# Seven quadrant products in both layers' output projections of a two-layer hybrid trunk on one core

## The chip, the core and the metric

The kernel runs on one core of a Trainium2 chip. The metric is the time of one execution in device microseconds (us), the median of several runs. The engines of the core run their own instruction queues side by side: TensorE (PE; PEld is its weight load), VectorE (DVE), ScalarE (ACT), GpSimd (POOL) and SyncE (SP, which here issues most DMA transfers; POOL issues a few).

## The reference

x is 512 tokens x 1024, fp32, and two layers run one after the other. Cut to what matters:

```python
def hybrid_layer(x, ...):
    h = rmsnorm(x, norm_g)
    p = h @ w_in                                  # 1024 x 3488
    (cq, ckv, kr, g_a, c_h, c_b, c_c, g_b, sg_u, sg_v, g_c, mq, mk, mv, g_d) = split(p)
    o_a = latent attention of cq, ckv, kr         # MLA, 4 heads
    o_b = c_b * short_conv(c_c * c_h, conv_w)
    o_c = spatial_gate(sg_u, sg_v, ...)
    o_d = block-sparse attention of mq, mk, mv    # MoBA, 4 heads
    y = concat([o_a * silu(g_a), o_b * silu(g_b), o_c * silu(g_c), o_d * silu(g_d)])
    return y @ w_out                              # 1024 x 1024

for l in range(2):
    x = x + hybrid_layer(x, ...)
```

The change concerns the last product, y @ w_out, and what leads from it into the next layer's h.

## The kernel before, in words

**Products.** An fp32 product is made of three passes in a rounded format (fp32r): each operand is split into a high part and a low rest, and `mm3` (L253) adds hi·hi, hi·lo and lo·hi into one accumulator. ACT makes the high part (a copy), DVE the low one (a subtraction): `split2` (L246). The activations stand transposed, features on the 128 partitions and the 512 tokens along the row: hT (tags hh0, hl0, hh1, hl1: two halves of 1024 features, each high and low) for the input projection, and y in eight tiles of 128 features x 512 tokens (`y_tiles`, L834): tiles 0 and 1 come from MLA, 2 and 3 from the convolution, 4 and 5 from the spatial gate, 6 and 7 from MoBA.

**Weights.** They are cut into units of 512 KB (`add_unit`, L295). `load_units` (L357) loads them on the SP queue into two raw buffers and `split_units` (L372) splits each in two halves of 128x512 into six pairs of split buffers (`whi`, `wlo`), in the order of use and up to four units ahead of it.

**Order of work.** Nothing is scheduled by the compiler. At build time a planner (`Order`, L66) runs coroutines: the main one (`main`, L1306) emits PE's matmuls and advances a modelled time, and chains spawned by it (`Chain`, L150) emit the work of ACT, DVE, POOL and the transfers when the modelled time of their inputs has come. What it emits is a fixed program order for each engine; on the chip each engine then goes through its own queue in order. A buffer is taken from `Slots` (L112) and given back, an `Event` holds a chain until another has passed a point. So an edit in one place shifts the order on all engines.

**One layer.** PE runs first the low-rank columns (tile cq, 4 token tiles), then `SEQ` (L335): sq (spatial gate's v and MoBA's q), ga0, ga1, kv (MoBA's k and v), su0 to gc1 (the features of convolution, gates and spatial gate). Between these matmuls stand the heads of MLA and MoBA (`mla_heads`, L1120; `moba_heads`, L1166), each with its transposes, scores and outputs. Then comes the output projection.

**Output projection, layer 0.** Eight products, tile "o": for each half of the 1024 output columns and each of the four token tiles, eight y tiles of three passes into one accumulator of 128x512: 2 x 4 x 8 x 3 = 192 matmuls of 128x512. After a token tile's second half `out_chain` (L1237) adds the residual, starts the sum of squares for the next norm and spawns `pre_norm` (L589) of the next layer, which scales the row by its norm (DVE, tile h), transposes it on PE (tile hT, 4 transposes per half) and splits it into hTh and hTl.

**Output projection, layer 1.** Seven products (`seven`, L1328), the method of Strassen and Winograd on 2 x 2 quadrants: y's quadrants are token halves (columns 0:256 and 256:512 of a y tile) by feature halves (`K0` = tiles 2, 3, 0, 1 and `K1` = 4, 5, 6, 7), w_out's quadrants b11, b12, b21, b22 are feature halves by halves of the output columns. `ZPROD` gives the order: b11, t3, b21, t4, t2, t1, b22, each named for its weights; t1 to t4 are sums of weight quadrants. Each product has two row blocks of four feature tiles of three passes: 24 matmuls of 128x512, 168 in all, in the tiles oz, ox, oy, and ot for the last row block. What it needs beside:
- weight sums: `t_sums` (L316) copies a quadrant within DRAM (8 copies of 512 KB on SP, L322) and adds another onto it (8 accumulating transfers issued by POOL, L328). It is spawned for layer 1 when layer 0's MLA heads are done (end of `mla_heads`).
- sums of y quadrants: `put_y` (L838) subtracts the two token halves of a K0 tile in place (DVE), so that t3's left operand stands in the tile, and stores every y tile in DRAM (`ysc`). `s_chain` (L855), once for each pair of a K0 and a K1 tile, loads both back, makes three sums of 256 columns on DVE (tiles ys) and splits them into `sums`: S for t2, S4 for b22 (one pair of tiles with 512 columns) and S for t1 (a second pair with 256 columns). These lie in the buffers of hT, which is free by then.
- outputs: `z_out` (L1276) adds or subtracts a product to or from the residual rows (DVE), and `row_done` (L1257) ends a row: in layer 1 the store.

**Parameters.** `load_params` (L522) loads a layer's small vectors (norm gains, convolution weights and so on) in 14 transfers on SP, `load_norm_gain` (L513) the gain of the input norm. Layer 1's are loaded in the middle of layer 0's projection, after the first group of token tiles.

**Waiting between layers.** `pre_norm` of layer 1 writes hT only after `h_done` of layer 0, an event set when layer 0 no longer needs the buffers of hT.

Of the kernel before, what the change touches and what calls it, by code (L numbers as in the profile page):

```python
# [18 lines left out]
P = 128  # L19
# [180 lines left out]
def hybrid_trunk(ctx: ExitStack, tc: tile.TileContext, x, positions, norm_g, w_c, w_f, w_t, w_o, mla_q_norm_g,  # L200
# [115 lines left out]
    def t_sums(l):  # L316

        for steps in ((("t1", "b11", "b12"), ("t3", "b12", "b22")), (("t2", "t1", "b22"),), (("t4", "t2", "b21"),)):
            for n, a, _ in steps:
                for j in range(2):  # L320
                    o.clk["D"] = max(o.clk["D"], o.now) + 1500.0
                    nc.sync.dma_start(z_src(l, n, j), z_src(l, a, j))  # L322
                    yield o.now + 4000.0
            yield o.now + 4000.0
            for n, _, b in steps:
                for j in range(2):
                    o.clk["G"] = max(o.clk["G"], o.now) + 1000.0
                    nc.gpsimd.dma_start(z_src(l, n, j), quad(l, b, j), accum_op=ALU.add, max_dma_last_dim=1024)  # L328
                    yield o.now + 4000.0
            yield o.now + 8000.0  # L330

# [25 lines left out]
    def load_units():  # L357
        for u in order:
            ch = Chain(o)
            u.raw_slots = rawS  # L360
            if u.name in ("c2_0", "c3_0") or u.name[:-3] in ZPROD and u.name[-3] == "1":
                u.raw_slots = tkS
                u.raw = (yield from tkS.get(ch, f"raw_{u.name}", 96)).rearrange("p a b c -> p (a b c)")
            else:
                u.raw = yield from rawS.get(ch, u.name)
            dma(ch, P * u.a * u.b * 4, u.raw[:, :u.a * u.b], u.src)
            o.set(u.loaded, ch.t)
            for e in LOAD_HOOKS.pop(u.name, ()):
                e()
            yield o.now  # L370
# [179 lines left out]
    for l in range(DEPTH):  # L550
        L = Layer()
        L.l = l
        L.ng_ev = Event()
        L.hT = [[Event(), Event()] for _ in range(NT)]
        L.xss = [cst.tile([P, 4], F32, name=f"xss{t}_{l}") for t in range(NT)]
        L.qd = [Event() for _ in range(NT)]
        L.kd = [Event() for _ in range(NT)]
        L.stat = [Event() for _ in range(NT)]
        L.Vt, L.Mt, L.gates, L.gate_ev, L.MD = {}, {}, {}, {}, {}
        L.md_ev = {n: [Event() for _ in range(NT)] for n in ("mq", "mk", "mv")}  # L560
        L.vt_ev = [Event() for _ in range(NT)]
# [6 lines left out]
        L.hT_free, L.h_done, L.h = Event(), Event(), {}  # L568
# [20 lines left out]
    def pre_norm(L, t, xx, t0, release):  # L589
# [18 lines left out]
        def half(c):  # L608
            c2 = Chain(o, tps[c])
            tp = yield from trS.get(c2, f"hT{t}_{c}_{L.l}")  # L610
            for k in range(4):
                kt = c * 4 + k
                yield from c2.pe(109.0, PE.transpose, tp[:, k * P:(k + 1) * P], h[:, kt * P:(kt + 1) * P], ident)
            hput(c2)
            if L.l:
                yield from c2.wait(layers[L.l - 1].h_done)
            if c not in L.h:
                L.h[c] = [big.tile([P, 4, S], F32R, tag=f"h{x}{c}", name=f"hT{x}{c}_{L.l}") for x in "hl"]
            yield from split2(c2, *(z[:, :, t * P:(t + 1) * P] for z in L.h[c]), tp.rearrange("p (k n) -> p k n", k=4))
            trS.put(c2)  # L620
            o.set(L.hT[t][c], c2.t)
# [216 lines left out]
    def put_y(ch, L, kt, yv):  # L838
# [16 lines left out]
    def s_chain(L, kk):  # L855

        ch = Chain(o)
        for kt in (K0[kk], K1[kk]):
            yield from ch.wait(L.y[kt])
            ch.t = max(ch.t, L.left["y", kt])  # L860
        yield from ch.wait(L.hT_free)
        w = []
        for kt in (K0[kk], K1[kk]):
# [3 lines left out]
        a, b = w  # L867
        ch.t = max(ch.t, c2.t)
        yield from ch.dve(V.tensor_tensor, b[:, 256:512], b[:, 256:512], a[:, 256:512], op=ALU.add)
        yield from ch.dve(V.tensor_tensor, b[:, 0:256], b[:, 0:256], b[:, 256:512], op=ALU.subtract)  # L870
        c2 = Chain(o, ch.t)
        yield from ch.dve(V.tensor_tensor, a[:, 0:256], a[:, 0:256], b[:, 256:512], op=ALU.subtract)
# [32 lines left out]
    def gc_chain(j):  # L905
        def f(L, a, t0):
# [4 lines left out]
            t2S.put(ch)  # L911
        return f


# [205 lines left out]
    def mla_heads(L):  # L1120
# [116 lines left out]
    def out_chain(L, half, t, a, t0, c0=0, c1=512):  # L1237
# [10 lines left out]
        elif half == 1:  # L1248
# [57 lines left out]
    def main():  # L1306
# [20 lines left out]

        def seven(L):  # L1328
            l = L.l
            L.sums = [[big.tile([P, 4, n], F32R, tag=f"h{x}{i}", name=f"sum{x}{i}_{l}") for x in "hl"]  # L1330
                      for i, n in enumerate((512, 256))]
            o.set(L.hT_free, o.now + PELAT)
            us = {}

            def left(n, kk, i):
                c = i * P
                if n in ("t2", "b22"):
                    z, ev = [y[:, kk, (256 if n == "t2" else 0):] for y in L.sums[0]], L.s[n][kk]
                elif n == "t1":
                    z, ev = [y[:, kk, :] for y in L.sums[1]], L.s[n][kk]  # L1340
                else:
                    kt = (K0 if n in ("b11", "t3") else K1)[kk]
                    z, ev = [y[:, (256 if n in ("t3", "t4") else 0):] for y in y_tiles(L, kt)], L.y[kt]
                return z[0][:, c:c + P], z[1][:, c:c + P], ev

            def prod(n, i, a, first, c0=0, c1=512):
# [20 lines left out]
            for n in ZPROD:  # L1367
                for i in range(2):
# [25 lines left out]
            o.set(L.h_done, o.now)  # L1394

        early_put(m)
        for L in layers:
# [19 lines left out]
            for n in SEQ:  # L1417
                if n in TOKS:
                    us = []
                    for t in range(NT):  # L1420
# [17 lines left out]
            if L.seven:  # L1438
                yield from seven(L)
            else:  # L1440
                o.set(L.h_done, o.now)
            for half in range(0 if L.seven else 2):
                us = {}

# [43 lines left out]
    def start():  # L1488
# [52 lines left out]
        hS.put(ch)  # L1541
        o.set(L0.ng_ev, ch.t)

    o.spawn(start())
    o.run()

# [49 lines left out]
```

## Time and profile before

| what | value |
|---|---|
| median of 3 runs | 502.64 us (502.39 to 503.83) |
| the profiled execution's own time | 504.06 us |
| its span in the trace | 502.4 us, so 1.66 us lie outside the span |
| mean granted TensorE clock | 0.999 |
| DMA | 67.30 MB in 28267 packets, mean 134 GB/s |
| transfers on the hardware queue | 37.1% of 16 engines' span |
| transfers issued by POOL | 5.8% of 16 engines' span |

How to read the profile. The page gives each engine's busy time and its share of the span, then the span in 40 slices of 12.56 us, one digit for the busy tenths of each. The chain that ended last is followed back from the last instruction to whatever released it; its shares by engine say which engine set the time. The waits list an engine's idle time by what ended it. Groups of instructions are given by line, engine, operation and tile (out<-in), with the number of instructions, the busy time, the mean ns of one, and the idle time ahead of them. Since the helpers issue nearly everything, the line is mostly that of a helper (L161 for ACT, DVE and POOL, L187 for PE, L264 for loads), and the tile's name tells the work apart. The windows give each engine's busy time between two moments.

### The profile page before, as it was taken

To read this page: it belongs to the slowest core of one execution; us is meant where nothing else is said; L and a number is where in the kernel's file an instruction comes from. 1 tells how busy PE (TensorE), PEld (TensorE's weight loads), DVE (VectorE), ACT (ScalarE), POOL (GpSimd) and SP (SyncE) were. 2 spreads that over 40 slices of the span, in tenths; PEclk is the share of its full clock that TensorE was granted. 3 is DMA by queue.
4 is the path that set the end of the run, shared out by engine and by line. 5 is a ranking of instruction groups with operands and counts; after the bars stand their busy time and mean duration, and the time that the engine had idled before them with its cause. 6 is when DMAs were issued, how large, how long until landed. Compare 5 with 4: busy or idle time off the path is not lost.

```text
span 502.4 us, 7746 instructions
## 1 busy us (share of the span) xinstructions
PE 492.6 (98%) x2472; PEld 417.1 (83%) x2472; DVE 368.7 (73%) x958; ACT 307.2 (61%) x913; POOL 145.8 (29%) x329
## 2 busy tenths in 40 slices
PE   6899999999999999999999999999999999999997
PEld 3798888888888888888889988888888888888886
DVE  4877985458888888544466889777878888765982
ACT  4788755556687766433346896566767587524640
POOL 5867884454011100100311458532240000000000
PEclk9999999999999999999999999999999999999999
DMA  7543414111277722965854422230115312465752
GB/s 266 151 138 99 134 63 142 46 65 43 61 233 207 172 84 88 289 214 165 202 179 130 127 85 84 85 127 1 64 56 180 102 43 105 173 246 185 267 171 89
DMA packets 28267, 67.30 MB, mean 134 GB/s; under 512 B 6593, under 2 KB 11969, under 8 KB 28098
## 3 DMA queue, kind: packets, MB, share of 16 engines
q1 hardware_dynamic: 23970, 62.61, 37.1%
q0 software_dynamic: 4256, 4.20, 5.8%
q8 instruction: 19, 0.31, 0.2%
q14 instruction: 22, 0.18, 0.1%
HBM read 60.51 MB, written 14.68 MB: 150 GB/s over the span
## 4 chain that ended last, share of the span: by engine, by line
PE 91%; POOL 3%; DVE 2%; DMA 2%; ACT 1%; issue 1%; POOLq 0%; DVEq 0%
PE kv L187 10%; PE o L187 9%; PE cq L187 6%; PE sq L187 5%; PE cc L187 4%; PE gb L187 4%; PE cb L187 4%; PE gd L187 4%; PE ch L187 4%; PE su L187 4%; PE gc L187 4%; PE sa L187 3%; PE ga L187 3%; PE oy L187 3%; PE ox L187 2%; PE oz L187 2%
## 5 line engine op out<-in xcount | busy, mean ns | idle before, releaser
L161 ACT ACTIVATE pha<-pTa 128x512 fp32r<-128x512 f32 (+3 forms) x32 | 13.9, 434 | 21.0 <-PE pTa L187 20.8
L161 ACT ACTIVATE pa<-pa,mna 128x256 f32<-128x256 f32 (+3 forms) x45 | 23.9, 539 | 4.1 <-DVE mna L161 4.0
L187 PE MATMUL kv<-whi_kv,hTh 128*128 128x512 f32 x64 | 26.0, 406 | 0.0
L161 ACT ACTIVATE pd<-pd,mnd 128x256 f32<-128x256 f32 (+3 forms) x46 | 24.5, 546 | 1.2 <-DVE mnd L161 0.8
L187 PE MATMUL kv<-whi_kv,hTl 128*128 128x512 f32 x64 | 25.1, 392 | 0.0
L161 ACT ACTIVATE phd<-pTd 128x512 fp32r<-128x512 f32 (+3 forms) x32 | 13.9, 436 | 18.2 <-PE pTd L187 18.0
L187 PE MATMUL kv<-wlo_kv,hTh 128*128 128x512 f32 x64 | 24.9, 390 | 0.0
L187 PE MATMUL cq<-whi_c,hTh 128*128 128x416 f32 x64 | 23.8, 372 | 0.9 <-ACT hTh L161 0.9
L187 PE MATMUL cq<-whi_c,hTl 128*128 128x416 f32 x64 | 22.6, 353 | 0.1
L187 PE MATMUL cq<-wlo_c,hTh 128*128 128x416 f32 x64 | 22.4, 351 | 0.0
L161 DVE CUSTOM_DVE_ANT_0 pa<-sa,maskb 128x512 f32<-128x512 f32 (+3 forms) x32 | 15.0, 484 | 8.2 <-PE pTa L187 5.1
L328 POOL DMA_DIRECT2D t<-in_w_o_dram x8 | 8.8, 1153 | 37.3 <-DMA t<-t 37.2
L161 ACT ACTIVATE hTh<-hT 128x512 fp32r<-128x512 f32 x16 | 9.3, 597 | 16.7 <-PE hT L187 16.6
L187 PE MATMUL sq<-yTh,hTh 128*128 128x512 f32 x48 | 18.9, 393 | 0.0
L187 PE MATMUL o<-whi_wo,yTh 128*128 128x512 f32 x48 | 18.8, 391 | 0.0
L187 PE MATMUL sq<-yTh,hTl 128*128 128x512 f32 x48 | 18.7, 390 | 0.0
L187 PE MATMUL sq<-yTl,hTh 128*128 128x512 f32 x48 | 18.7, 390 | 0.0
L187 PE MATMUL o<-whi_wo,yTl 128*128 128x512 f32 x48 | 18.7, 389 | 0.0
L187 PE MATMUL o<-wlo_wo,yTh 128*128 128x512 f32 x48 | 18.7, 389 | 0.0
L161 DVE TENSOR_TENSOR pld<-pTd,phd 128x512 fp32r<-128x512 f32 (+3 forms) x32 | 15.4, 486 | 4.3 <-ACT phd L161 4.0
L161 DVE TENSOR_TENSOR pla<-pTa,pha 128x512 fp32r<-128x512 f32 (+3 forms) x32 | 15.4, 484 | 4.1 <-ACT pha L161 3.9
L161 DVE CUSTOM_DVE_ANT_0 pd<-sd,maskb 128x256 f32<-128x256 f32 (+3 forms) x32 | 15.1, 484 | 1.0 <-PE pTd L187 0.8
(385 smaller groups left out, 1823.2 us busy)
## 6 DMA issues: line engine op xcount, KB each, us to landing
raw_sq<-in_w_t_dram SPq DMA_DIRECT2D x8, 512.0 KB, 3.5
raw_kv<-in_w_t_dram SPq DMA_DIRECT2D x8, 512.0 KB, 3.5
t<-in_w_o_dram POOLq DMA_DIRECT2D x8, 512.0 KB, 8.1
raw_wo<-in_w_o_dram SPq DMA_DIRECT2D x8, 512.0 KB, 3.6
raw_t<-t SPq DMA_DIRECT2D x8, 512.0 KB, 3.6
raw_c<-in_w_c_dram SPq DMA_DIRECT2D x8, 416.0 KB, 4.1
raw_b<-in_w_o_dram SPq DMA_DIRECT2D x6, 512.0 KB, 4.1
raw_ga<-in_w_f_dram SPq DMA_DIRECT2D x4, 512.0 KB, 3.6
```

Of the source, the lines that this page charges most:

```text
L161: f(*a, **k)
L187: f(*a, **k)
L328: nc.gpsimd.dma_start(z_src(l, n, j), quad(l, b, j), accum_op=ALU.add, max_dma_last_dim=1024)
```

## The change

- `SEVEN` becomes (0, 1): layer 0's output projection runs as seven products too. With it layer 0 gets 14 weight units for its projection (8 before), its weight sums, its y-tile stores and sums, and its output rows end in the order of `z_out`; layer 1's first tiles (`torder`) go in the order 2, 3, 0, 1.
- Layer 0's weight sums are spawned at 36 us of the planner's time (`TS0`), layer 1's after layer 1's sq, no longer at the end of layer 0's MLA heads. A weight unit that reads a sum waits in the planner for that sum (`tsum_ev`).
- y tile 5, the last to be made, is used in place: it is not stored in DRAM and loaded back, its own tile goes to `s_chain` (`own`).
- The sums of `s_chain` lie in one pair of tiles (t1's in columns 0:256, t2's in 256:512). b22's left operand S4 is split into the place of A11 (columns 0:256 of the K0 tiles), which b11 alone has read, after b11 (event `p1`). So one half of the hT buffers is not used in the projection.
- `h_done` is one event for each half of hT: the half that the sums do not use is free from the start of the seven products, the other after t1.
- Layer 1's parameters are loaded when layer 0's cc1 has made its convolution (`next_params`), no longer in the middle of the projection; the gain of the input norm is loaded after t3.

```diff
-SEVEN = (1,)
+SEVEN = (0, 1)
+TS0 = 36000.0
...
+    tsum_ev = {(l, n, j): Event() for l, n in tsum for j in range(2)}
...
                     nc.gpsimd.dma_start(z_src(l, n, j), quad(l, b, j), accum_op=ALU.add, max_dma_last_dim=1024)
+                    o.set(tsum_ev[l, n, j], o.now + 10000.0)
...
+            key = (int(u.name[-1]), u.name[:-3], ord(u.name[-3]) - 48)
+            if key in tsum_ev:
+                yield from ch.wait(tsum_ev[key])
             dma(ch, P * u.a * u.b * 4, u.raw[:, :u.a * u.b], u.src)
...
-                yield from c2.wait(layers[L.l - 1].h_done)
+                yield from c2.wait(layers[L.l - 1].h_done[c])
...
         if L.seven:
-            nc.sync.dma_start(ysc[L.l][kt], yv)
-            ch.t = max(ch.t, t0 + 3000.0)
-            L.left["y", kt] = ch.t
             if kt in K1:
-                o.spawn(s_chain(L, K1.index(kt)), None, 3)
+                o.spawn(s_chain(L, K1.index(kt), yv if kt == 5 else None, t0), None, 3)
+            if kt != 5:
+                nc.sync.dma_start(ysc[L.l][kt], yv)
+                ch.t = max(ch.t, t0 + 3000.0)
+                L.left["y", kt] = ch.t
...
+    def s_chain(L, kk, own, t0):
+        ch = Chain(o, t0)
+        kts = (K0[kk],) if own is not None else (K0[kk], K1[kk])
...
+        a, b = w if own is None else (w[0], own)
...
-        yield from split2(c2, *(z[:, kk, :] for z in L.sums[0]), b)
+        yield from split2(c2, *(z[:, kk, :] for z in L.sums), a)
         t2S.put(c2)
-        for n in ("t2", "b22"):
+        for n in ("t2", "t1"):
             o.set(L.s[n][kk], c2.t)
-        yield from split2(ch, *(z[:, kk, :] for z in L.sums[1]), a[:, 0:256])
+        yield from ch.wait(L.p1)
+        yield from split2(ch, *(z[:, 0:256] for z in y_tiles(L, K0[kk])), b[:, 0:256])
         t2S.put(ch)
-        o.set(L.s["t1"][kk], ch.t)
+        o.set(L.s["b22"][kk], ch.t)
...
-        if L.l == 0:
-            for l in SEVEN:
-                if l:
-                    o.spawn(t_sums(l), None, 4)
...
+    def next_params(L):
+        ch = Chain(o)
+        yield from ch.wait(L.b_ev[1][1])
+        load_params(layers[L.l + 1])
...
-            L.sums = [[big.tile([P, 4, n], F32R, tag=f"h{x}{i}", name=f"sum{x}{i}_{l}") for x in "hl"]
-                      for i, n in enumerate((512, 256))]
+            L.sums = [big.tile([P, 4, 512], F32R, tag=f"h{x}0", name=f"sum{x}_{l}") for x in "hl"]
+            o.set(L.h_done[1], o.now)
...
+                if n == "b11":
+                    o.set(L.p1, o.now + PELAT)
+                if n == "t1":
+                    o.set(L.h_done[0], o.now)
                 if n == "t3" and l + 1 < DEPTH:
                     o.spawn(load_norm_gain(layers[l + 1]))
-                    load_params(layers[l + 1])
...
+                    if n == "sq" and l and L.seven:
+                        o.spawn(t_sums(l), None, 4)
                     if n == "kv":
                         o.spawn(load_residual(L), None, 3)
+                        if L.seven and l + 1 < DEPTH:
+                            o.spawn(next_params(L), None, 3)
...
+    if 0 in SEVEN:
+        o.spawn(t_sums(0), TS0, 4)
     o.spawn(start())
```

More of the change, by code (lines that the diff above doesn't have):

```diff
@@ L567, in hybrid_trunk @@
         L.seven = l in SEVEN
-        L.hT_free, L.h_done, L.h = Event(), Event(), {}
+        L.hT_free, L.p1, L.h_done, L.h = Event(), Event(), [Event(), Event()], {}
         L.s = {n: [Event() for _ in range(4)] for n in ("t2", "t1", "b22")}
@@ L848, in put_y @@
         if L.seven:
-            nc.sync.dma_start(ysc[L.l][kt], yv)
-            ch.t = max(ch.t, t0 + 3000.0)
-            L.left["y", kt] = ch.t
             if kt in K1:
-                o.spawn(s_chain(L, K1.index(kt)), None, 3)
-    def s_chain(L, kk):
-        ch = Chain(o)
-        for kt in (K0[kk], K1[kk]):
+                o.spawn(s_chain(L, K1.index(kt), yv if kt == 5 else None, t0), None, 3)
[6 more added lines that the diff above has]
+        kts = (K0[kk],) if own is not None else (K0[kk], K1[kk])
+        for kt in kts:
             yield from ch.wait(L.y[kt])
             ch.t = max(ch.t, L.left["y", kt])
-        yield from ch.wait(L.hT_free)
+        if own is None:
+            yield from ch.wait(L.hT_free)
         w = []
-        for kt in (K0[kk], K1[kk]):
+        for kt in kts:
             w.append((yield from t2S.get(ch, f"ys{kt}_{L.l}")))
@@ L866, in s_chain @@
             dma(c2, P * 2048, w[-1], ysc[L.l][kt])
-        a, b = w
+        a, b = w if own is None else (w[0], own)
         ch.t = max(ch.t, c2.t)
-        yield from ch.dve(V.tensor_tensor, b[:, 256:512], b[:, 256:512], a[:, 256:512], op=ALU.add)
-        yield from ch.dve(V.tensor_tensor, b[:, 0:256], b[:, 0:256], b[:, 256:512], op=ALU.subtract)
+        yield from ch.wait(L.hT_free)
+        yield from ch.dve(V.tensor_tensor, a[:, 256:512], b[:, 256:512], a[:, 256:512], op=ALU.add)
+        yield from ch.dve(V.tensor_tensor, a[:, 0:256], a[:, 0:256], a[:, 256:512], op=ALU.subtract)
         c2 = Chain(o, ch.t)
-        yield from ch.dve(V.tensor_tensor, a[:, 0:256], a[:, 0:256], b[:, 256:512], op=ALU.subtract)
-        yield from split2(c2, *(z[:, kk, :] for z in L.sums[0]), b)
+        yield from ch.dve(V.tensor_tensor, b[:, 0:256], b[:, 0:256], a[:, 256:512], op=ALU.subtract)
+        yield from split2(c2, *(z[:, kk, :] for z in L.sums), a)
         t2S.put(c2)
-        for n in ("t2", "b22"):
+        for n in ("t2", "t1"):
             o.set(L.s[n][kk], c2.t)
-        yield from split2(ch, *(z[:, kk, :] for z in L.sums[1]), a[:, 0:256])
+        yield from ch.wait(L.p1)
+        yield from split2(ch, *(z[:, 0:256] for z in y_tiles(L, K0[kk])), b[:, 0:256])
         t2S.put(ch)
-        o.set(L.s["t1"][kk], ch.t)
+        o.set(L.s["b22"][kk], ch.t)
     def su_chain(j):
@@ L910, in f @@
             yield from finish(ch, L, 4 + j, L.u[j], tg)
-            t2S.put(ch)
+            if not (L.seven and j == 1):
+                t2S.put(ch)
         return f
@@ L1336, in left @@
                 c = i * P
[L1337 to L1340, printed above, removed]
-                else:
-                    kt = (K0 if n in ("b11", "t3") else K1)[kk]
-                    z, ev = [y[:, (256 if n in ("t3", "t4") else 0):] for y in y_tiles(L, kt)], L.y[kt]
+                if n in ("t2", "t1"):
+                    z, ev = [y[:, kk, (256 if n == "t2" else 0):] for y in L.sums], L.s[n][kk]
+                else:
+                    kt = (K0 if n in ("b11", "t3", "b22") else K1)[kk]
+                    z = [y[:, (256 if n in ("t3", "t4") else 0):] for y in y_tiles(L, kt)]
+                    ev = L.s[n][kk] if n == "b22" else L.y[kt]
                 return z[0][:, c:c + P], z[1][:, c:c + P], ev
@@ L1390, in seven @@
                                       slot[b].put if n in ("b21", "t4", "b22") else None))
+                if n == "b11":
+                    o.set(L.p1, o.now + PELAT)
+                if n == "t1":
+                    o.set(L.h_done[0], o.now)
                 if n == "t3" and l + 1 < DEPTH:
                     o.spawn(load_norm_gain(layers[l + 1]))
-                    load_params(layers[l + 1])
-            o.set(L.h_done, o.now)
         early_put(m)
@@ L1440, in main @@
             else:
-                o.set(L.h_done, o.now)
+                for ev in L.h_done:
+                    o.set(ev, o.now)
             for half in range(0 if L.seven else 2):
```

## The prediction

> **What bounds the kernel now.** I read the page from the top: the busy times, the slices, and the share of each engine in the chain that ended last.
>
> ```profile
> span 502.4 us, 7746 instructions
> PE 492.6 (98%) x2472; PEld 417.1 (83%) x2472; DVE 368.7 (73%) x958; ACT 307.2 (61%) x913; POOL 145.8 (29%) x329
> PE   6899999999999999999999999999999999999997
> POOL 5867884454011100100311458532240000000000
> PE 91%; POOL 3%; DVE 2%; DMA 2%; ACT 1%; issue 1%; POOLq 0%; DVEq 0%
> ```
>
> TensorE (PE) is busy 492.6 of 502.4 us. Its row is below 9 only in the first two slices (the start) and the last one (the end). What PE waits for is then asked of the waits, core-wide:
>
> ```profile
> PE hT L187 <- DVE h L161: 3.0, 3, 1.3
> PE warm L1496 <- DVE ones L161: 1.3, 1, 1.3
> PE cq L187 <- ACT hTh L161: 0.9, 1, 0.9
> PE cT L187 <- DVE ct L161: 0.6, 1, 0.6
> ```
>
> These four (total us, count, largest) make 5.8 us, and belong to the start. From there on PE is a closed row of matmuls: every us of matmul that goes is a us of time, if all that feeds PE keeps up; and every us by which something comes late is a us lost.
>
> The two places where the change does its work are the output projections. From the chain of waits, in order of time (start, us, engine, tile):
>
> ```profile
> 215.33 32.64 PE o L187 x144
> 247.97 0.87 PE hT L187 x8
> 254.51 5.47 PE o L187 x24
> 460.48 5.44 PE oz L187 x24
> 482.24 13.60 PE oy L187 x60
> ```
>
> "o" is layer 0's projection in eight products, oz and oy belong to layer 1's, in seven. One 128x512 matmul costs 32.64/144 = 0.2267 us in layer 0, and 5.44/24 = 13.60/60 = 0.2267 us in layer 1. The seven-product form has no slower matmul.
>
> **The change part by part.**
>
> *Seven products in layer 0.* Eight products are 8 x 24 = 192 matmuls, seven are 168. The instruction orders of the two programs differ on PE by just these 24 of 128x512. 24 x 0.2267 = **5.44 us** less, all of it on the path, since PE is closed there. [...]
>
> What the seven products add lies on DVE, ACT and the queues: six more weight units to split (14 for 8), y-tile sums, subtractions and output additions. The stages, by engine (us; busy of PE, PEld, DVE, ACT, POOL; clock; DMA share; GB/s):
>
> ```profile
> 215.20:261.30 46.10, 46.10 (x217) 38.36 (x216) 23.47 (x38) 15.92 (x35) 6.09 (x10) 1.00 0.68 188
> 460.50:471.40 10.90, 10.90 (x49) 9.02 (x49) 9.49 (x19) 7.72 (x15) 0.00 (x0) 1.00 0.88 297
> 471.40:482.20 10.80, 10.80 (x49) 8.94 (x48) 10.80 (x22) 6.37 (x13) 0.00 (x0) 1.00 0.76 258
> 482.20:493.10 10.90, 10.90 (x50) 9.03 (x49) 6.89 (x12) 2.21 (x4) 0.00 (x0) 1.00 0.34 115
> 261.30:272.00 10.70, 10.70 (x63) 10.06 (x62) 9.21 (x20) 6.63 (x20) 2.75 (x4) 1.00 0.50 173
> ```
>
> Layer 1 already runs seven products. In its second third DVE is busy 10.80 of 10.80 us, and PE still 10.80 of 10.80: the buffers ahead carry it. So seven products alone fit beside PE. Layer 0 has more to do in that stage, namely the next layer's h:
>
> ```profile
> L161 DVE TENSOR_TENSOR wlo_t<-raw_t,whi_t 128x512 fp32r<-128x512 f32 x16 | 10.6, 684 | 0.0
> L161 ACT ACTIVATE whi_t<-raw_t 128x512 fp32r<-128x512 f32 x16 | 9.3, 619 | 3.5 <-DMA raw_t<-t 3.5
> L161 DVE SCALAR_TENSOR_TENSOR h<-xr,xss,ng 128x512 f32<-128x512 f32 x8 | 6.2, 793 | 3.8 <-POOL xss L161 3.8
> L161 DVE TENSOR_TENSOR hTl<-hT,hTh 128x512 fp32r<-128x512 f32 x16 | 10.8, 682 | 3.9 <-ACT hTh L161 3.9
> ```
>
> Six more units are 12 halves: 12 x 0.684 = 8.2 us of DVE and 12 x 0.619 = 7.4 us of ACT. The three windows of layer 1 hold 9.49 + 10.80 + 6.89 = 27.2 us of DVE in 32.6 us. The first two row tiles of the next h that fall in this stage put 4 x 0.793 + 4 x 0.682 = 5.9 us on top (four halves scaled, four transposed groups split): 33.1 in 32.6. But PE's seven products take 168 x 0.2267 = 38.1 us, and both the last 5.5 us of them and the first 10.70 us of layer 1, where DVE now has 9.21, take some of it. I count DVE as just fitting, **0 us** on the path, with up to 5.9 us if its work comes at the wrong time (rival A). Below zero is excluded: PE has no wait here to win back.
>
> *Head chains.* The projection starts with b11 on y tiles 2, 0, 1, 3, where it took 2, 3, 0, 1 first before; the tiles of the last heads, 6 and 7, are wanted by b21, a third product, 10.9 us on (460.50 to 471.40 in layer 1). The last heads' output transposes are at
>
> ```profile
> 202.25 0.27 PE L187 MATMUL od<-pld,Mt 128*128 128x128 f32 x1
> 434.51 0.27 PE L187 MATMUL od<-pld,Mt 128*128 128x128 f32 x1
> ```
>
> which leaves 215.33 - 202.25 = 13 us in layer 0 and 460.48 - 434.51 = 26 us in layer 1 before they are late: 0 us.
>
> *Weight sums of layer 0.* The seven products need four quadrant sums of the weights, and these are eight copies by SP and eight accumulating transfers issued by POOL per layer. Those for layer 0 are new and stand in its first third; those for layer 1 move out of the end of layer 0 to behind layer 1's sq. The accumulating ones as they are now (us to issue: min, median, max; then to landing), and POOL and the other engines where they will stand:
>
> ```profile
> L328 POOL DMA_DIRECT2D t<-in_w_o_dram x8: 1005/1049/1505, 141.5 to 245.8; - x8
> DMA to landing us min/median/max: 5.8/8.1/9.6
> 200.83 1.00 POOL L328 DMA_DIRECT2D t<-in_w_o_dram  x1 [33.97 <-DMA t<-t]
> 125.00:150.00 25.00, 25.00 (x138) 21.37 (x137) 21.05 (x57) 19.09 (x46) 2.18 (x3) 1.00 0.50 142
> 150.00:180.00 30.00, 30.00 (x163) 25.42 (x162) 26.22 (x65) 22.21 (x53) 3.98 (x5) 1.00 0.69 182
> 64.00:80.00 16.00, 16.00 (x77) 13.29 (x76) 12.67 (x40) 9.03 (x28) 10.11 (x24) 1.00 0.22 70
> 80.00:97.30 17.30, 17.30 (x78) 14.26 (x77) 7.37 (x19) 8.24 (x32) 10.42 (x27) 1.00 0.28 89
> 80.49 0.61 POOL L161 TENSOR_TENSOR rbk<-krt,sinT 128x64 f32<-128x64 f32 x2 [4.82 <-DVE Q L161]
> 97.32 0.60 PE L187 MATMUL t0a<-ident,Q 128*96 128x128 f32 x4
> ```
>
> In POOL's new order four of layer 0's issues stand between the work of 64 and 80 us, ahead of the rotations of Q and of the shared key (80.49) and of the copy into K; the first head's transposes (97.32) wait for these. The other four stand at mq's ropes (about 108) and among the memsets of the second heads. At 1.05 us each, four issues are 4.2 us. POOL is idle 17.30 - 10.42 = 6.9 us between 80.00 and 97.30, 4.82 of it in one gap. The first transposes stand 21 matmuls earlier in PE's new order (21 x 0.2267 = 4.8 us), but several of Q's ropes have gone over to DVE, which has 17.30 - 7.37 us free. I take **0 us**; the other end is rival B. Each issue also waits for its copy. One such wait was 33.97 us long; it came from a copy late in SP's queue, with nothing behind it on POOL. Now there is something behind, so the SP queue counts: the copies stand behind these loads,
>
> ```profile
> 42.40 5.99 SPq L264 DMA_DIRECT2D raw_ga<-in_w_f_dram x2
> 85.85 0.33 SPq L264 DMA_DIRECT2D raw_cc<-in_w_f_dram x1
> DMA to landing us min/median/max: 4.5/4.7/5.7
> ```
>
> t1 by raw_ga and t2 by raw_cc, and 4.5 to 5.7 us to land is over 10 us before POOL comes to each: 0 us. Layer 1's eight issues stand between mk's ropes, where POOL has gaps of 5 us:
>
> ```profile
> 336.06 0.19 POOL L161 TENSOR_SCALAR mmk<-mmk 128x4 f32<-128x4 f32 x1 [5.72 <-ACT junk L161]
> ```
>
> 0 us for these as well.
>
> *Last y tile in place, S4 in A11's place, h_done in two.* One store and one reload of 256 KB per layer fall away; S4's split waits for the end of b11, which PE has left 20 us before b22 wants it. The sums use one pair of h tiles instead of two, so the other pair takes the next layer's h during b22. All of this only brings something forward, on engines that aren't the bound: 0 us. It would cost what rival A costs if this cover were gone.
>
> *Parameters loaded ahead.* Fourteen issues of the SP queue move from the middle of layer 0's projection to about cc1:
>
> ```profile
> 222.84 1.08 SPq L525 DMA_DIRECT2D cg_b<-in_mla_q_norm_g_dram  x1
> 228.49 1.53 SPq L538 DMA_DIRECT2D cw<-in_conv_w_dram  x3
> ```
>
> From 222.84 to 230.02 they hold SP for 7.2 us; at their new place the weight loads behind them are held by as much, at DMA shares of 0.50 to 0.69. Weights are loaded at least a unit ahead (5.44 us of PE each and more); 0 us, at most 7.2 - 5.4 = 1.8.
>
> *Sum.* 502.4 - 5.44 = 496.96 us of span. The profiled execution took 504.06 us, 1.66 beyond its span, so the same execution after would take 498.6. It lies 1.42 above the median of the three runs, 502.64, and the median is what is predicted: 502.64 - 5.44 = **497.2 us**.
>
> **The rivals.**
>
> *A, DVE late in layer 0's projection or at its seam.* The 5.9 us of h on top of a full DVE (10.80 of 10.80) come just where t2's and t1's left sums and t21's weights are split, and b22 or the first cq waits. For it: 33.1 in 32.6 above. Against: sums and weights are made ahead, and layer 1's full stretch cost PE nothing. Half of the 5.9 us lost gives 497.2 + 3.0 = 500.2; span of the case 498.6 to 501.1.
>
> *B, slower: POOL held at the new issues.* An issue by POOL in 64-80 us may take longer than the 1.0 to 1.5 us of the rows, whose surroundings had DVE at 21.05/25 = 84% and 26.22/30 = 87%. [...] It decides from d per issue with 4d - 6.9 > 5.44 + 1.5, that is d = 3.5 us. Against: the rows at 84 and 87% show 1.5 at most, so the mechanism isn't seen. [...]
>
> *C, no gain: the change does not do what it says.* The 24 matmuls go, but PE then waits for what it didn't outrun before: the heads, 13 and 26 us ahead, or the weight sums. The 5.44 us turn into waits and it stays at 502.6. For it: every engine's order is rebuilt by the planner. Against: all margins named are more than twice 5.44, except DVE's.
>
> **How the numbers follow.** A measurement of this kernel can tell about 0.3%, 1.5 us, from no change. Forecast 497.2 (496.2 to 498.6): 0.72. A, about 500.2 (498.6 to 501.1): 0.13. C, about 502.6: 0.08. B, about 509: 0.07. Faster by over 0.3% (below 501.1) is forecast and A, 0.85; same is C, 0.08; slower is B, 0.07. The range takes in the forecast and A: 496.2 (1 us under, the spread of the runs and of the start) to 500.9; C and B are left out, 0.15.
>
> **What would show it.** Right: PE's busy time falls by 5.4 us to about 487, 24 fewer 128x512, layer 0's projection 38.1 us plus transposes, waits of PE still about 6 us. A: waits of PE on hT, oy or cq for DVE's or ACT's tiles between 210 and 280 us. B: POOL's issues at 64-80 us over 3.5 us each, and PE waiting for t0a's Q or K. C: PE waits for od, Mt or for wlo_t. The forecast is wrong if PE's waits grow by more than 1.4 us, wherever they stand.

## The result and the profile after

| | before | after |
|---|---|---|
| median, measured side by side | 503.01 us (502.39 to 503.83, 4 runs) | 498.92 us (498.08 to 499.12, 4 runs) |
| ratio | | 0.9915 (0.9895 to 0.9934) |
| profiled execution, its span | 504.06 us, 502.4 | 499.12 us, 497.4 |

4.09 us are gained; 5.44 were forecast (497.2 us). The changed kernel was measured twice more, each time beside the kernel before: ratios 0.9916 (0.9902 to 0.9929) and 0.9912 (0.9898 to 0.9925). A ratio is not exactly the quotient of the two medians: in the second measurement the medians, 499.49 and 503.15 us, would give 0.9927. Where a difference in us is worked out from two ratios below, it is their difference times 503 us.

The page of the changed kernel, its span, busy times and the slices of PE and DVE, then PE's waits (total us, count, largest):

```profile
span 497.4 us, 7832 instructions
PE 486.4 (98%) x2448; PEld 412.5 (83%) x2448; DVE 386.0 (78%) x1008; ACT 317.0 (64%) x933; POOL 156.2 (31%) x328
PE   6899999999999999999999999999999999999997
DVE  4877884777988788669898698677969788765992
```
```profile
PE hT L188 <- DVE h L162: 3.9, 3, 2.2
PE warm L1516 <- DVE ones L162: 1.3, 1, 1.3
PE t0a L188 <- DVE Q L162: 1.1, 1, 1.1
PE cT L188 <- DVE ct L162: 0.6, 1, 0.6
PE mp L188 <- ACT vnh L162: 0.3, 1, 0.3
PE ng L188 <- DMA gz<-in_norm_g_dram: 0.2, 1, 0.2
```

PE has 24 matmuls fewer (2448 for 2472) and is still the engine that is always busy. DVE has become fuller, 78% for 73%. The six lines make 7.4 us. New among the waits behind the start are t0a (1.1 us) and mp (0.3 us), both in layer 0 and both far from the output projection.

Where the time went is read from four matmuls that stand in both traces: the first of ga and of the output projection, in layer 0 and in layer 1. Before:

```profile
65.74 0.39 PE L187 MATMUL ga<-hTh,whi_ga 128*128 128x512 f32 x1
215.17 0.39 PE L187 MATMUL o<-whi_wo,yTh 128*128 128x512 f32 x1
310.84 0.39 PE L187 MATMUL ga<-hTh,whi_ga 128*128 128x512 f32 x1
460.32 0.39 PE L187 MATMUL oz<-whi_b,yTh 128*128 128x512 f32 x1
```

and after:

```profile
64.81 0.39 PE L188 MATMUL ga<-hTh,whi_ga 128*128 128x512 f32 x1
216.24 0.39 PE L188 MATMUL oz<-whi_b,yTh 128*128 128x512 f32 x1
306.44 0.39 PE L188 MATMUL ga<-hTh,whi_ga 128*128 128x512 f32 x1
455.55 0.39 PE L188 MATMUL oz<-whi_b,yTh 128*128 128x512 f32 x1
```

| stretch | before | after | difference |
|---|---|---|---|
| start to ga | 65.74 | 64.81 | -0.93 |
| ga to layer 0's projection | 149.43 | 151.43 | **+2.00** |
| layer 0's projection to layer 1's ga | 95.67 | 90.20 | **-5.47** |
| layer 1's ga to its projection | 149.48 | 149.11 | -0.37 |
| layer 1's projection to the end of the span | 42.08 | 41.85 | -0.23 |

The stretch that holds the seven products gave 5.47 us, the forecast 5.44. The first stretch is a matter of the execution: over all traces of this study ga began between 64.33 and 65.85 us. What was not forecast are the 2.00 us ahead of the projection, 1.13 of them one wait for t0a and 0.27 one for mp.

The projection itself ran with a full DVE and without a wait (columns as in the windows of before):

```profile
226.00:241.00 15.00, 15.00 (x68) 12.43 (x67) 15.00 (x30) 9.79 (x21) 0.00 (x0) 1.00 0.63 224
```

DVE is busy 15.00 of 15.00 us there, PE too. That is rival A's place, with no room left and nothing lost.

The wait at t0a is read backwards through three engines. ACT, DVE and POOL of the changed kernel (start, us, operation, idle time before it and what ended it):

```profile
84.92 1.16 ACT L162 ACTIVATE whi_su<-raw_su 128x512 fp32r<-128x512 f32 x2 [6.05 <-DMA raw_su<-in_w_f_dram]
```
```profile
85.58 0.69 DVE L162 TENSOR_TENSOR wlo_su<-raw_su,whi_su 128x512 fp32r<-128x512 f32 x1 [5.33 <-ACT whi_su L162]
86.19 0.22 DVE L162 TENSOR_TENSOR Q<-Q,rbq 128x64 f32<-128x64 f32 x1
```
```profile
78.84 1.01 POOL L330 DMA_DIRECT2D t<-in_w_o_dram  x1
87.30 1.10 POOL L162 TENSOR_TENSOR rbk<-krt,sinT 128x64 f32<-128x64 f32 x2 [7.45 <-DVE Q L162]
```

ACT idles 6.05 us for the load of raw_su; DVE stands at the same unit's low part, with the last step of the rotation of Q next in its queue; POOL idles 7.45 us for that Q, with the shared key and K behind it. POOL had finished its own issue at 79.85, so it is not what held the chain. That Q stands behind this unit on DVE is new, too. In the kernel before DVE did the step ahead of the unit, where a late raw_su could not hold it:

```profile
79.98 0.35 DVE L161 TENSOR_TENSOR Q<-Q,rbq 128x64 f32<-128x64 f32 x2
80.96 1.42 DVE L161 TENSOR_TENSOR wlo_su<-raw_su,whi_su 128x512 fp32r<-128x512 f32 x2 [0.62 <-ACT whi_su L161]
```

The load (us to landing) and the window of 76.5 to 85 us in which it was in flight (share of the DMA engines and GB/s last), first of the kernel before, then of the changed one:

```profile
raw_su<-in_w_f_dram SPq DMA_DIRECT2D x1, 512.0 KB, 3.5
```
```profile
76.50:85.00 8.50, 8.50 (x39) 7.04 (x38) 5.91 (x14) 4.39 (x10) 4.18 (x9) 1.00 0.60 173
```
```profile
raw_su<-in_w_f_dram SPq DMA_DIRECT2D x1, 512.0 KB, 8.3
```
```profile
76.50:85.00 8.50, 8.50 (x39) 7.05 (x38) 2.88 (x9) 1.39 (x4) 3.07 (x5) 1.00 1.12 234
```

The same load took 8.3 us instead of 3.5, with the DMA engines' share at 1.12 instead of 0.60, beside the accumulating transfers that POOL issued at 66.9 to 78.8 us.

### The profile page after: what moved, and what is told of

The parts are those of the page before. It is cut to its first block, busy times and chain, and to the rows that moved or that the text cites. A ratio compares the mean times of both kernels' runs of the same rounds, so it can differ in the third digit from the quotient of the medians.

```text
span 497.4 us, 7832 instructions
## 1 busy us (share of the span) xinstructions
PE 486.4 (98%) x2448; PEld 412.5 (83%) x2448; DVE 386.0 (78%) x1008; ACT 317.0 (64%) x933; POOL 156.2 (31%) x328
## 4 chain that ended last, share of the span: by engine, by line
PE 87%; POOL 4%; ACT 3%; DMA 3%; DVE 2%; issue 1%; POOLq 0%; DVEq 0%
PE kv L188 7%; PE cq L188 6%; PE oy L188 6%; PE sq L188 5%; PE cb L188 4%; PE gd L188 4%; PE ch L188 4%; PE cc L188 4%; PE su L188 4%; PE gc L188 4%; PE gb L188 4%; PE ox L188 4%; PE oz L188 4%; PE sa L188 3%; PE ga L188 2%; PE od L188 2%
## 5 line engine op out<-in xcount | busy, mean ns | idle before, releaser
L162 ACT ACTIVATE pd<-pd,mnd 128x256 f32<-128x256 f32 (+3 forms) x50 | 26.9, 547 | 2.8 <-DVE mnd L162 2.3
L330 POOL DMA_DIRECT2D t<-in_w_o_dram x16 | 17.9, 1121 | 33.1 <-DMA t<-t 22.6
L162 ACT ACTIVATE pa<-pa,mna 128x256 f32<-128x256 f32 (+3 forms) x40 | 21.4, 542 | 2.5 <-DVE mna L162 2.4
L162 DVE TENSOR_TENSOR wlo_t<-raw_t,whi_t 128x512 fp32r<-128x512 f32 x32 | 21.1, 691 | 0.0
L162 ACT ACTIVATE whi_t<-raw_t 128x512 fp32r<-128x512 f32 x32 | 18.2, 618 | 4.1 <-DMA raw_t<-t 4.1
L162 POOL TENSOR_SCALAR xss<-xss 128x1 f32<-128x1 f32 x8 | 3.8, 476 | 52.3 <-ACT jk L162 45.1
L162 DVE TENSOR_TENSOR wlo_b<-raw_b,whi_b 128x512 fp32r<-128x512 f32 x24 | 16.0, 688 | 0.7 <-ACT whi_b L162 0.7
```

The lines of the kernel that those rows point to most:

```text
L162: f(*a, **k)
```

## The experiments

Theory 1: the traffic of layer 0's first four accumulating transfers delays raw_su, and through DVE and POOL the first head. Theory 2: POOL's issuing time does (rival B in small). Theory 3: the plan placed t0a 21 matmuls earlier than Q can be ready. Beside these, each part that had been priced at nothing was undone by itself. Kernels that were not measured side by side are compared by their ratios to the kernel before, which ran beside each of them.

**e1: the sums' bytes taken away, the order kept.** The accumulating transfers carry 16 KB each, so layer 0's weight sums lack most of their second term.

```diff
+                    if l == 0:
+                        nc.gpsimd.dma_start(z_src(l, n, j)[0:P, 0:32], quad(l, b, j)[0:P, 0:32], accum_op=ALU.add, ...)
+                    else:
                         nc.gpsimd.dma_start(z_src(l, n, j), quad(l, b, j), accum_op=ALU.add, max_dma_last_dim=1024)
```

> Same order of work; the eight accumulating transfers of layer 0's weight sums are issued by POOL as before but carry 16 KB each and not 512 KB (so layer 0's weight sums lack most of the second term). Theory 1 (traffic: the accumulating transfers of 66 to 84 us make raw_su land in 8.3 us and not 3.5, DVE's queue stands behind its split, Q's rope is late, and PE waits 1.1 us for t0a): raw_su lands in under 5 us, the wait at t0a goes, 497.5 us (1.1 to 1.4 under the changed kernel's 498.9). Theory 2 (POOL's issuing time itself delays the ropes) and theory 3 (the plan placed t0a 21 matmuls earlier than Q can be ready): the wait at t0a stays about 1 us, 498.9 us.

Measured: 498.27 us, ratio 0.9896 (0.9883 to 0.9909). The load, the same window and the first head in its trace:

```profile
raw_su<-in_w_f_dram SPq DMA_DIRECT2D x1, 512.0 KB, 3.4
```
```profile
76.50:85.00 8.50, 8.50 (x40) 7.02 (x39) 5.77 (x15) 4.42 (x10) 4.78 (x11) 1.00 0.52 154
```
```profile
92.93 0.60 PE L188 MATMUL t0a<-ident,Q 128*96 128x128 f32 x4
```

raw_su lands in 3.4 us, t0a runs without a wait at its early place, and POOL still issues eight transfers of nearly a us each. Theory 1 holds in the trace. POOL's issues (theory 2) and the early place of t0a (theory 3) make no wait by themselves. That the new order takes part is not excluded: it put t0a 21 matmuls, 4.8 us, earlier and Q behind raw_su on DVE, and in the old order a landing 5 us late might have cost nothing. No run has the old order with the transfers beside raw_su. The ratio is 0.002 lower, 1 us, than the changed kernel's 0.9915, but the two intervals overlap.

**e9 and e12: two transfers moved, and the control.** In e9 t3's two accumulating transfers are issued after the copy into K. All other engines have the same order, instruction by instruction.

```diff
+                    if l == 0 and n == "t3":
+                        late.append((z_src(l, n, j), quad(l, b, j)))
+                    else:
                         nc.gpsimd.dma_start(z_src(l, n, j), quad(l, b, j), accum_op=ALU.add, ...)
...
         yield from ch.pool(G.tensor_copy, L.K[:, :, :, 64:96], ...)
+        for dst, src in late:
+            nc.gpsimd.dma_start(dst, src, accum_op=ALU.add, max_dma_last_dim=1024)
```

> t3's two accumulating transfers of layer 0 are issued by POOL after the copy into K and not before the rotations of Q and the shared key; the order of PE, DVE, ACT and SP is the same instruction by instruction. Theory 1 (their traffic beside raw_su makes it land in 7 to 8.3 us and PE wait 0 to 1.1 us at t0a): raw_su lands in under 6 us, no wait at t0a in the trace, 0.5 to 1 us under the changed kernel of the same call. Rival (the first pair alone is enough, or the wait has to do with the order): raw_su as late as before, the same time.

> The changed kernel once more, as the control of this call: 498.9 to 499.5 us, a wait at t0a between 0 and 1.2 us.

Measured: e9 498.24 us (ratio 0.9907, 0.9893 to 0.9921), the unchanged control 498.24 us (0.9912, 0.9898 to 0.9925). The load came down to 3.9 us, as theory 1 says:

```profile
raw_su<-in_w_f_dram SPq DMA_DIRECT2D x1, 512.0 KB, 3.9
```

but nothing was gained over the control, because the control did not wait either: raw_su took 6.5 us in its trace,

```profile
raw_su<-in_w_f_dram SPq DMA_DIRECT2D x1, 512.0 KB, 6.5
```

and t0a ran on time. So the wait is a matter of the execution.

**e5: the changed kernel again.**

> The changed kernel itself, unchanged, beside the kernel before and the other kernels of this call: 498.9 us again, 4.1 to 4.5 under the kernel before. Its trace tells whether the wait of 1.1 us at t0a comes in each execution: raw_su landed 8.3 us after its issue in the first trace, 7.0 us in a kernel with the same transfers where PE did not wait. If the wait is a matter of the execution, it lies between 0 and 1.2 us here.

Measured: 499.49 us (ratio 0.9916, 0.9902 to 0.9929), with raw_su at 7.7 us and a wait of

```profile
94.40 0.31 PE L188 MATMUL t0a<-ident,Q 128*96 128x128 f32 x1 [0.51 <-DVE Q L162]
```

Over the three traces of the same kernel, raw_su at 6.5, 7.7 and 8.3 us goes with waits of 0, 0.51 and 1.13 us. Four more kernels (e4, e8, e10 and e11 below) have the same order on every engine up to there: raw_su at 7.0 us (e4) makes no wait, at 7.2 and 7.3 (e10, e11) the first four transposes take 0.86 us and not 0.60, and at 7.6 (e8) the wait is 0.41 us. The slack is about 7 us of landing time. Between the waiting trace and the one that did not wait, the stretch from ga to the projection is 151.43 against 150.10 us; 0.67 us over the kernel before remain in the latter, 0.28 of it the wait at mp (e1 has it too, so it is not the sums' traffic), and the rest was not taken apart.

**e2, e6, e7: the sums at other places.**

```diff
-TS0 = 36000.0
+TS0 = 100000.0        # e2;  24000.0 in e6,  60000.0 in e7
```

> Layer 0's weight sums are spawned at 100 us of the plan and not at 36, behind the first heads; t0a then stands 21 matmuls later in PE's order, where it stood before the change. Theories 1, 2 and 3 all take away the wait at t0a (1.1 us) and the one at mp (0.3 us): 497.5 us. If the sums' traffic only collides elsewhere, or if the lost 1.4 us come from the start or from the output projection, it stays at 498.9 us.

> Layer 0's weight sums are spawned at 24 us of the plan and not at 36. The first four accumulating transfers then stand some 10 us earlier on POOL, away from the load of raw_su, and t0a stands in PE's order where it stood before the change. Theory 1 (traffic beside raw_su costs 1.1 us): no wait at t0a, 497.5 to 498.3 us. Rival (the sums' copies then collide with the loads of the start, whose DMA share is already 0.9 in the first slices): new waits before 65 us, 499 us or more.

> Layer 0's weight sums are spawned at 60 us of the plan: behind the rotation of the shared key, but 40 us of the plan before the place that cost 4 us. Theory: that place was slow because t4's sum landed at 217 us, SP's queue stood at the load of raw_t that needs it, the reloads of the y tiles stood behind, and DVE then had no room up to b22. If so, it depends on how late t4's sum is: here it stands before the second heads' memsets again, so the z stage is as in the changed kernel, and the wait at t0a is gone: 497.5 to 498.3 us. If lateness of the sums costs by degrees: 499.5 to 501 us.

Measured: e2 502.97 us (ratio 0.9996, 0.9983 to 1.0009), e6 501.61 us (0.9966, 0.9955 to 0.9977), e7 501.05 us (0.9958, 0.9943 to 0.9972). All three lost the wait at t0a, and by their ratios all three were slower than the changed kernel: I expected 497.5 to 498.3 in the main. Each got other waits. In e2, three, of which two stand in the projection:

```profile
183.54 0.33 PE L188 MATMUL pTd<-ident,pd 128*128 128x128 f32 x1 [2.06 <-DVE pld L162]
235.97 0.50 PE L188 MATMUL ox<-wlo_t,yD 128*128 128x512 f32 x1 [0.90 <-DVE wlo_t L162]
247.35 0.47 PE L188 MATMUL oy<-whi_t,sumh 128*128 128x512 f32 x1 [1.69 <-DVE xr L162]
```

On its SP queue and on its DVE,

```profile
217.27 0.32 SPq L265 DMA_DIRECT2D raw_t<-t  x1
217.64 6.75 SPq L265 DMA_DIRECT2D ys<-ysc  x6
```
```profile
226.72 0.42 DVE L162 TENSOR_TENSOR ys<-ys,ys 128x256 f32<-128x256 f32 x1 [2.24 <-DMA ys<-ysc]
```

raw_t stands until the last sum lands (SP waits 4.8 us for it), the reloads of the y tiles stand behind it, and DVE, idle for 2.24 us where it has none to spare, runs full up to 247 us and is late for the last products. That is rival A, made by a late sum. At pTd PE waits 1.15 us in e6 and 1.73 in e7 too; ACT stood 3.37 and 2.93 us just before, for the store of a y tile whose buffer is used again. Which of the shifted orders made the store late was not taken apart, and neither were e6's other waits (hTl 1.1, mp 0.8, oz 0.3 us). In e7 the wait in the trace is not what cost the time: the traced execution took 499.65 us at a granted clock of 1.000, another one 499.48, and the changed kernel beside them 499.49 in the median. The other four, at 0.993, took 500.87 to 502.41 us. No trace shows what brought their clock down.

**e3: layer 1 alone.**

```diff
-SEVEN = (0, 1)
+SEVEN = (1,)
```

> Seven products in layer 1 alone, as before the change, but with the rest of it: last y tile in place, S4 in A11's place, layer 1's sums behind its sq. Layer 0 has its 192 matmuls again and no weight sums. If the gain is the 24 matmuls less the wait at the first heads and nothing else: 498.9 + 5.4 - 1.4 = 502.9 us, the same as before the change (503.0). If the other parts bring something of their own: 502 us or less; if they cost: over 503.5.

Measured: 503.33 us, ratio 1.0001 (0.9992 to 1.0009). This kernel keeps layer 1's part of the change (tile 5 in place, the sums in one pair of tiles, the weight sums behind sq), and that part is worth nothing, neither way. Layer 0's part is not in it: the parameters for layer 1 are loaded from 220.87 to 228.22 us, in the middle of layer 0's projection as before. Its stretch from layer 0's projection to layer 1's ga is 95.66 us, that of the kernel before 95.67 and of the changed one 90.20, so the gain comes with layer 0's 24 matmuls.

**e8: the parameters back after t3.**

```diff
                 if n == "t3" and l + 1 < DEPTH:
                     o.spawn(load_norm_gain(layers[l + 1]))
+                    load_params(layers[l + 1])
...
-                        if L.seven and l + 1 < DEPTH:
-                            o.spawn(next_params(L), None, 3)
```

> Layer 1's parameters are loaded after t3 again, in the middle of layer 0's projection (14 issues on SP, 7.2 us). The prediction's view: moving them was worth 0, so 498.9 us. Rival: in the seven-product form SP has the reloads of the y tiles and of twice as many weight units there, 7.2 us of issues make them late, and DVE, which is full, has to catch up: PE waits for oy, sums or wlo_t between 225 and 250 us, 500.5 to 503 us.

Measured: 503.33 us, ratio 1.0004 (0.9986 to 1.0021), against 0.9916 of e5, measured beside it: 0.0088, 4.4 us (the medians lie 3.8 us apart). SP's queue, the matmul that waited, and the windows over the stall (PE's busy time and the clock):

```profile
228.01 0.42 SPq L531 DMA_DIRECT2D cg_b<-in_mla_q_norm_g_dram  x1
...
232.75 1.53 SPq L544 DMA_DIRECT2D cw<-in_conv_w_dram  x3
234.32 0.94 SPq L265 DMA_DIRECT2D ng<-in_norm_g_dram  x2
235.36 0.94 SPq L265 DMA_DIRECT2D raw_t<-t  x2
```
```profile
246.87 0.77 PE L188 MATMUL oy<-whi_t,sumh 128*128 128x512 f32 x1 [3.50 <-DVE xr L162]
```
```profile
242.00:244.00 2.00, 1.36 (x7) 0.78 (x5) 1.57 (x3) 1.89 (x4) 0.00 (x0) 1.00 0.79 322
244.00:246.00 2.00, 0.00 (x0) 0.00 (x0) 2.00 (x4) 1.33 (x3) 0.00 (x0) 0.92 0.67 189
246.00:248.00 2.00, 1.13 (x3) 0.97 (x4) 1.92 (x4) 1.25 (x4) 0.00 (x0) 0.50 0.13 49
248.00:250.00 2.00, 2.00 (x7) 1.52 (x6) 1.38 (x2) 2.00 (x6) 0.00 (x0) 0.50 0.71 213
250.00:252.00 2.00, 2.00 (x6) 1.61 (x5) 0.00 (x0) 0.08 (x1) 0.00 (x0) 0.50 0.00 0
```

The parameters hold SP from 228.01 to 234.28, raw_t is issued 19.4 us after the projection's start (216.00) and not 15.3 as in e5, DVE splits it late, and PE stands 3.50 us. With the stall comes a second loss in this trace: the granted clock falls to 0.50 and for about 6 us the matmuls stand 0.43 us apart and not 0.2267. The times of the other executions go the same way: the four at a clock of 1.000 took 501.51 to 502.42 us, the five at 0.993 (the traced one among them) 502.62 to 505.27, and the three at 0.997 503.93 to 505.85. So roughly half of the 4.4 us, an estimate from 501.7 against e5's 499.49, is the wait alone.

**e4: both halves of hT held to the end.**

```diff
-            o.set(L.h_done[1], o.now)
...
-                if n == "t1":
-                    o.set(L.h_done[0], o.now)
...
+            for ev in L.h_done:
+                o.set(ev, o.now)          # after the last product
```

> The split of h_done undone: both halves of layer 1's hT are written only when layer 0's seven products have all been issued, as a single event at their end. The prediction's view (it only brings something forward, cover for DVE at the seam): with the cover gone PE waits at the seam for the first transposes' splits (0.62 on ACT, 0.68 on DVE, twice, and DVE has four tiles to make up), 2 to 4 us: 501 to 503 us, with waits of PE on hTh, hTl or hT around 252 to 262 us. Rival (it is hidden anyway): 498.9 us.

Measured: 501.50 us, ratio 0.9958 (0.9943 to 0.9974): 0.0043 or 2.2 us over the changed kernel's 0.9915. The trace has the wait where it was expected, at the seam, on DVE:

```profile
256.63 0.63 PE L188 MATMUL hT<-ident,h 128*128 128x128 f32 x4 [1.49 <-DVE hTl L162]
```

**e10: y tile 5 through DRAM again.**

```diff
-                o.spawn(s_chain(L, K1.index(kt), yv if kt == 5 else None, t0), None, 3)
-            if kt != 5:
+                o.spawn(s_chain(L, K1.index(kt), None, t0), None, 3)
+            if True:
...
```

> Only the in-place use of y tile 5 undone: it is stored in DRAM and loaded back in both layers, as the other y tiles. The prediction's view: 0. Rival: its reload is the last one in SP's queue and s_chain's last sums become late for a DVE that is full from 226 to 241 us, PE waits in oy, 0.5 to 3 us. With the parameters' 6 us in mind I expect the rival in part: 499.5 to 501 us.

Measured: 498.44 us, ratio 0.9912 (0.9899 to 0.9926), the control's 0.9912. Nothing: my expectation was wrong, the prediction's 0 right.

**e11: layer 1's sums at their old place.**

```diff
-                    if n == "sq" and l and L.seven:
-                        o.spawn(t_sums(l), None, 4)
...
         o.set(L.mla_ev, o.now)
+        if L.l == 0:
+            o.spawn(t_sums(1), None, 4)
```

> Only the place of layer 1's weight sums undone: they are spawned at the end of layer 0's MLA heads again, so their copies and accumulating transfers stand beside layer 0's last heads and its seven products. If the place matters (SP and the DMA engines are at 0.9 to 1.0 in the first 5 us of that stage): waits of PE in oz to oy, 500.5 to 503 us. If not: 499 us.

Measured: 501.15 us, ratio 0.9966 (0.9955 to 0.9977), 0.0054 or 2.7 us over the control. Two waits in the projection, behind a stretch in which the DMA engines' share is 1.16:

```profile
221.00:226.00 5.00, 5.00 (x23) 4.14 (x23) 4.18 (x11) 3.65 (x8) 0.00 (x0) 1.00 1.16 454
226.00:231.00 5.00, 3.76 (x16) 2.48 (x15) 5.00 (x11) 3.56 (x8) 1.01 (x1) 1.00 0.57 205
```
```profile
228.81 0.50 PE L188 MATMUL oz<-wlo_b,yD 128*128 128x512 f32 x1 [1.24 <-DVE wlo_b L162]
245.23 0.47 PE L188 MATMUL oy<-whi_t,sumh 128*128 128x512 f32 x1 [1.39 <-DVE xr L162]
```

## Why the prediction was right, and where it was not

*Seven products in layer 0, -5.44 us.* Right in mechanism and size: 5.47 us in the stretch that holds them, and e3, with layer 0's eight products, has none of it.

*What they add on DVE, 0 us.* Right for the changed kernel, which shows no wait from 216 to 262 us. The count said that DVE just fits, and it is literally so: 15.00 of 15.00 us. With so little margin small displacements bring rival A about: in e2, e4, e8 and e11 PE's waits in the projection or at its seam end on tiles of DVE (wlo_t, xr, hTl, wlo_b), and the kernels are 2.2 to 4.4 us slower, where 3 had been given for A.

*Weight sums of layer 0, 0 us.* This is the step that was wrong, though the range held the result. It asked whether the sums come in time for those who need them, and whether POOL's issues hold POOL; both were answered rightly. It did not ask what 2 MB of accumulating traffic does to a weight load that happens to be beside it. raw_su landed in 6.5 to 8.3 us for 3.5, and where that exceeded about 7 us, PE waited up to 1.13 us at t0a. The prediction reckoned with the 21 matmuls by which t0a moves forward and answered them with the free time of DVE; it did not see that a step of Q's ropes now stood behind the split of that load. The rows show SP's load and POOL's transfers in flight together, with the engines' share at 1.12 and not 0.60; how the ones held up the other no run here shows.

*Parameters loaded ahead, 0 us and at most 1.8.* Right as a term of the sum, since it compares with a kernel in which they cost nothing: neither the kernel before nor e3, which leaves them in the projection, has a wait of PE there. Wrong as a statement on that part: with seven products in place, loading them after t3 costs 4.4 us (e8). The bound of 1.8 us had been worked out from the weights being a unit ahead; it left out that DVE, busy 15.00 of 15.00 us, has no room to make up a late load there, and it knew nothing of a loss like the one behind the stall of 3.50 us in e8's trace, where the granted clock was 0.50 for about 6 us.

*Layer 1's sums, 0 us.* The same: 2.7 us if they stay where they were (e11). *h_done in two*: the prediction said that without this cover it costs what rival A costs; 2.2 us. *Tile 5 in place*: 0, confirmed by e10.

*Head chains, 0 us.* Nothing was late in the last heads. The first head of layer 0 was, for the reason above.

*Rival B* is out, and no run shows an issue by POOL of the length that its 509 us stands on: the sixteen of the changed kernel took

```profile
L330 POOL DMA_DIRECT2D t<-in_w_o_dram x16: 1006/1093/1624, 66.9 to 415.6; - x16
```

1.1 us each in the median and 1.62 at most, with DVE at 12.80 of 16 us from 64 to 80 us, and not 3.5. *Rival C* did not come.

Of the 1.72 us between forecast and median, 0.37 are the kernel before, measured at 503.01 and no longer 502.64. The other 1.35 are of the size of the waits at t0a and mp, 1.13 + 0.27 us, in the one execution that was traced; that pair of traces differs by 4.94 us of time, since its first stretch is 0.93 us shorter. In the third measurement, where t0a did not wait in the trace, the difference was 502.95 - 498.24 = 4.71 us.

By the prediction's own marks the result is less clean than the number. 498.92 us lies above 498.6, where its interval for the forecast ends and that of rival A begins, but A's mechanism did not occur: the loss has a cause that no rival named, and that it stayed inside the range is in part luck. Its last sign, that PE's waits must not grow by more than 1.4 us, was crossed in the first trace (7.4 us for 5.8), mainly by t0a. In the traces of e5 and e12 the waits are 4.6 and 4.1 us, because those at the start are shorter there.

## What to carry to other kernels

When a dense engine loses work, the saving is the number of instructions times their measured spacing (here 24 x 0.2267 = 5.44 us, and 5.47 came), and it arrives only as far as everything beside it still fits. A part of a change that removes nothing from the critical path can still be what lets the rest fit: price it also with the rest in place, not against the old kernel alone. And for each transfer that is moved, ask not only when it lands, but which loads are in flight beside it, which engine has a queue standing behind those loads, and how many us of slack they have.

## What the runs showed of the hardware

- With a stall of PE of 3.50 us in the middle of the kernel (e8, one trace) the granted clock was halved: 0.50 from 246 to 252 us, with matmuls of 128x512 spaced 0.43 us apart instead of 0.2267, 0.87 over 252 to 254 us and 1.00 over 254 to 256. Shorter waits left it at 1.00: 2.19 us in the changed kernel (it ended at 9.46 us; windows of 6 to 12 us), 1.69 us in e2 (it ended at 247.35 us; windows of 241 to 251 us). The 13 matmuls from 246.87 to 252.54 us took 5.67 us and not 2.95, so the stall cost 3.50 + 2.72 = 6.2 us, nearly twice its length. PE stood from 243.37 us, and the clock of 0.92 over 244 to 246 us, taken as one step from 1.00 to 0.50, puts the fall at about 245.7, an estimate: some 2.3 us into the wait.
- Beside accumulating transfers of 512 KB issued by POOL, a 512 KB load issued by SP took 6.5, 7.7 and 8.3 us in three executions of one program, and 3.5 us in the kernel before, which has none there; with 16 KB each the load took 3.4 us (e1), with two of the four moved away 3.9 us (e9).
